# Pads in three pools, so that the activations' parts lie 64 bytes from the weights' parts modulo 256

## The chip, the cores and the metric

The kernel runs on one core of a Trainium2 chip. The metric is the device time of the whole program, in microseconds; before the change three runs gave 2711.12, 2712.39 and 2712.43 us. About 0.2% (5.4 us) is what a measurement of this kernel can tell from no change.

## The reference, cut to what matters

Three transformer-like blocks follow one another on a sequence of 256 tokens with 1024 features, all in float32. Nearly all the work is matrix products of the 256 tokens with weights that are read once from HBM:

```
def first_block(x, c, ...):
    mod = silu(c) @ w_ada + b_ada
    h = modulate(rms_norm(x, g), shift, scale)
    p = h @ w_in                        # Fourier mixing, convolution, gates
    ...
    x = x + gate * ((gate_a * y_a + gate_b * y_b) @ w_o)
    x = x + gate * expert_choice_moe(...)   # 16 experts, 32 tokens each

def second_block(x, p, ...):
    ...                                  # LRU branch, sparse attention, merge
    x = x + (gelu(conv(xn @ w_up[:, :3072])) * (xn @ w_up[:, 3072:])) @ w_down
    x = x + sigmoid(rms(x) @ w_ple_gate) * (p @ w_ple_proj)

def third_block(x, ...):                 # two layers
    x = x + 0.5 * swiglu(rmsnorm(x), w_gu, w_down)      # 1024 -> 2*2816 -> 1024
    x = x + mixer(rmsnorm(x))            # sparse, then sliding-window attention
    x = x + 0.5 * swiglu(rmsnorm(x), w_gu, w_down)
```

## The kernel before, in words

**Products.** Activations are kept with features on the 128 partitions: a tile `[128, 8, 256]` holds 1024 features of 256 tokens, 1024 bytes in each partition for each of the 8 feature blocks. To keep float32 accuracy with the faster float32r matmul, each operand is split into a high part and a low part (`wh`, `wl` of the weights, `xh`, `xl` of the activations; names such as `xgh`/`xgl`, `hh`/`hl` are such pairs), and three matmuls replace one. `lin_fm` (feature-major result, most of the kernel) issues for each block `k` and each half `f` of a 256-column unit of weights

```
self.mm(o, wh[:, k, c], xh[:, k, :], ...)   # weights are loaded, tokens move
self.mm(o, wh[:, k, c], xl[:, k, :], ...)
self.mm(o, wl[:, k, c], xh[:, k, :], ...)
```

All go through `mm` (L394). Each is a weight load of 128 columns (LDWEIGHTS, shown as PEld) and a matmul that streams 256 columns of the other operand; the load for the next matmul overlaps the stream of the current one. A unit of 1024 x 256 weights is 48 matmuls. `lin_tm` (token-major result) has the roles exchanged: it loads the activations' parts and streams the weights' parts.

**Weights.** `Stream` brings weights from HBM into slots of 16384 bytes per partition (`raw`), and `prep_one` and `settle` (L280 on ScalarE, L289 on VectorE) split each unit into `wh` and `wl`, which lie side by side in another slot (`w`). The slots are pools on the right side of SBUF, allocated downwards; six serve the dense parts, ten the experts.

**Activations.** Their tiles come from pools that are opened and closed as on a stack, left ones upwards and right ones downwards. What counts for the change is where a tile begins in its partition. In the program as the allocator lays it out before the change (addresses modulo 256):

| pool | side | holds | modulo 256 |
|---|---|---|---|
| slots | right | `raw`, `w` (`wh`, `wl`), tiles lent for attention (`lent`) | 224 |
| `act` (L2623), under the slots | right | `xgh`/`xgl`, `hh`/`hl` of the feed-forward parts, `yh`/`yl`, `QS` | 224 |
| `fixed` (`kn.fx`) | left | parameters, `xT`, sums, identity `identr` (192) | various |
| `big` (L381), after `fixed` | left | `z0`/`z1`, `xg0`/`xg1`, `mt0`/`mt1`, the experts' `ht`, `xe` | 0 |
| `act2`, `plein`, where `big` has closed | left | `hh`/`hl` of one group of a feed-forward part, `pT` | 0 |
| `mods` (L825), then `one` (L827), after `big` | left | `one`: `hh`/`hl`, `ybh`/`ybl`, `uf` (96); `yf` (0) | 96 |
| `three` in the last mixer | left | `KH`/`KL` | 160 |

Tiles of the matrix kind have rows of 1024 bytes, slots are 16384 bytes apart, and the halves `c` of a weight row lie 512 bytes apart, so the difference between any block of an activation tile and any block of a weight tile is the same modulo 256. One case matters below: `yf` lies in the same region of SBUF as the `act` tiles do later (from byte 109312 on), but at 0 modulo 256.

**Order.** The program is emitted in the order of the work, with queues written out by hand: `step` emits the matmuls of a unit and then older evictions; `Stream.pump` issues the DMAs on SyncE as slots come free. A feed-forward part (`ffn`) emits gate and up units by groups of 1024 hidden features, then the down products (`acc`) of the group before. Of each feed-forward part, of which there are five, the group `g == 1` has its `hh`/`hl` in `act2`, the others in `act`.

Of the kernel before, what the change touches and what calls it, by code (L numbers as in the profile page):

```python
# [8 lines left out]
F32 = mybir.dt.float32  # L9
# [6 lines left out]
P = 128  # L16
# [333 lines left out]
class Kern:  # L350
# [24 lines left out]
    def open_act2(self, ctx):  # L375
        p = ctx.enter_context(self.pool("act2"))
        self.act2 = lambda name, dt=F32R: p.tile([P, 8, S], dt, name=name, tag="act2", bufs=2)

    def open_big(self, ctx):
        self.bigctx = ctx.enter_context(ExitStack())  # L380
        p = self.bigctx.enter_context(self.pool("big"))  # L381
        self.big = lambda name, i, dt=F32R: p.tile([P, 8, S], dt, name=name, tag=f"big{i}", bufs=1)
# [362 lines left out]
def plan_one(kn):  # L745
    st, A = kn.st, kn.A
    ph = 1
    u = kn.u1 = {}
    Wa = A["w_ada"][0]

    def ada(q, c):

        u["ada", q, c] = st.raw(ph, 2, 2048, Wa[:, q * 2048:(q + 1) * 2048].rearrange("(p k) n -> p k n", k=8)[:, 2 * c:2 * c + 2], 2 if q == 0 else 1)

    Wi = A["w_in"][0]
    for a in ADA[:3]:
        ada(*a)
    u["u", 0] = st.linear(ph, Wi, 0, 8, 0)
    ada(*ADA[3])
    u["u", 1] = st.linear(ph, Wi, 0, 8, 256)  # L760
    rest = ADA[4:]
    n = 0

    def more():
        nonlocal n
        n += 1
        if n in ADA_AT:
            ada(*rest.pop(0))

    for j in range(4):  # L770
        for nm, c0 in (("v", 512), ("c", 2560), ("b", 1536)):
            u[nm, j] = st.linear(ph, Wi, 0, 8, c0 + j * 256)
            more()
    for j in range(8):
        u["g", j] = st.linear(ph, Wi, 0, 8, 3584 + j * 256)
        more()
    for j in range(4):
        u["wf", j] = st.linear(ph, A["w_fourier"][0], 0, 4, j * 256)
        more()
        u["wc", j] = st.linear(ph, A["w_conv_out"][0], 0, 8, j * 256)  # L780
        more()
    for j in range(4):
        u["wo", j] = st.linear(ph, A["w_o"][0], 0, 8, j * 256)


def plan_experts(kn):
    st, A = kn.st, kn.A
    kn.ue = {}
    for e in range(16):
        for nm in ("w_gate_e", "w_up_e"):  # L790
            W = A[nm][0, e].rearrange("(c p i) n -> c p (i n)", p=P, i=4)
            if e < 2:
                kn.ue[e, nm] = [st.rows(2, 2, 2048, W[c][:, h * 4096:(h + 1) * 4096], pair=False) for c in range(2) for h in range(2)]
            else:
                kn.ue[e, nm] = [st.rows(2, 4, 2048, W[c]) for c in range(2)]
        W = A["w_down_e"][0, e].rearrange("(c p i) n -> c p (i n)", p=P, i=8)
        halves = [W[c][:, h * 4096:(h + 1) * 4096] for c in range(2) for h in range(2)]
        kn.ue[e, "w_down_e"] = d = []
        if e < 2:
            d += [st.rows(2, 4, 1024, w, pair=(e, n) == (1, 3)) for n, w in enumerate(halves)]  # L800
        elif e < 15:
            d += [st.rows(2, 8, 1024, W[c]) for c in range(2)]
        else:
            d += [st.rows(2, 4, 1024, w, pair=False) for w in halves[:3]]
            if 2 in kn.stages:
                plan_two_first(kn, 0)
            d.append(st.rows(2, 4, 1024, halves[3], (2,), pair=False))
    if 2 in kn.stages:
        plan_two_first(kn, 1)
# [13 lines left out]
def block_one(kn, outer):  # L823
    nc, A, st, V, SC, G = kn.nc, kn.A, kn.st, kn.V, kn.SC, kn.G
    modp = outer.enter_context(kn.pool("mods"))  # L825
    with ExitStack() as ctx:
        pool = ctx.enter_context(kn.pool("one"))  # L827
        st.phase = 1
# [606 lines left out]
def plan_two(kn):  # L1435
    st, A = kn.st, kn.A
    ph = 3
    if "e" not in kn.stages:
        plan_two_first(kn, 0)
        plan_two_first(kn, 1)  # L1440
    u = kn.u2
    W = A["w_in_2"][0]
    o_q, o_k, o_v, o_qi, o_ga, o_gb = 2048, 3072, 3328, 3584, 4168, 5192
    col = dict(q=(W, o_q), lx=(W, 0), lg=(W, 1024), ga=(W, o_ga), gb=(W, o_gb), qi=(W, o_qi), k=(W, o_k), v=(W, o_v), lb=(A["w_lru_br_2"][0], 0))

    def add(key):
        w, c = col[key[0] if isinstance(key, tuple) else key]
        u[key] = st.linear(ph, w, 0, 8, c + 256 * (key[1] if isinstance(key, tuple) else 0))

    add("k")  # L1450
    u["rg"] = st.unit(ph, 8, 256, [((0, P), (0, P), A["lru_wa_2"][0].rearrange("n c d -> c n d")),
                                   ((0, P), (P, 256), A["lru_wx_2"][0].rearrange("n c d -> c n d"))])
    u["middle"] = [("lx", 1), ("q", 0), ("lx", 2), ("ga", 0), ("lx", 3), ("q", 1), ("ga", 1), "v", ("q", 2), ("ga", 2), ("q", 3), ("ga", 3)]
    for key in u["middle"]:
        add(key)
    for j in range(4):
        add(("lg", j))
    u["later"] = [("gb", 0), ("gb", 1), ("lb", 0), ("lb", 1), ("lb", 2), ("lb", 3), ("gb", 2), ("gb", 3)]
    for key in u["later"]:
        add(key)  # L1460
    for j in range(4):
        u["ab", j] = st.linear(ph, A["w_attn_br_2"][0], 0, 8, j * 256)
    for j in range(4):
        u["wo", j] = st.linear(ph, A["w_out_2"][0], 0, 8, j * 256)
    kn.ffn2 = plan_ffn(st, ph, A["w_up_2"][0], 3072, A["w_down_2"][0])
    for j in range(4):
        u["pg", j] = st.linear(ph, A["w_ple_gate_2"][0], 0, 8, j * 256)
    u["pp"] = st.linear(ph, A["w_ple_proj_2"][0], 0, 2, 0, D)
# [458 lines left out]
def ple_input(kn, pool):  # L1927

    nc, A = kn.nc, kn.A
    pin = pool.tile([P, 2, 256], F32, name="pin")  # L1930
    nc.gpsimd.dma_start(pin, A["p_2"][0, 0].rearrange("(t p) n -> p t n", p=P))
    kn.pT = [pool.tile([P, 2, S], F32R, name=f"pT{i}") for i in range(2)]

    def run():
        for _ in range(4):
            yield
        ps = kn.psB("pT")
        for f in range(2):
            for t in range(2):
                kn.T.transpose(ps[:, f * 256 + t * P:f * 256 + (t + 1) * P], pin[:, t, f * P:(f + 1) * P], kn.ident)  # L1940
        yield
        kn.split(*kn.pT, ps.rearrange("p (a b) -> p a b", a=2))
    kn.bgs.append(run())
# [629 lines left out]
def start_at(kn, gain):  # L2573

    kn.st.phase = 3
    kn.st.pump()
    with kn.pool("start") as pool:
        setup(kn, pool)
        params(kn, 0)
        load_rows(kn, pool, 1, len(kn.used), kn.nc.gpsimd)  # L2580
        params(kn, 1)
        kn.SC.activation(kn.identr, kn.ident, AF.Copy)
        turn_x(kn)
        for _ in prepare_two(kn, pool):
            pass
    nx = Next(kn, gain, at=kn.two_parts("xg"))
    for j in range(4):
        nx.pair(j)
    return nx
# [20 lines left out]
def build(tc, A, out, stages=(1, "e", 2, 3)):  # L2610
    with ExitStack() as ctx:
        kn = Kern(ctx, tc, A, out, stages)
        if 1 in stages:
            plan_one(kn)
        if "e" in stages:
            plan_experts(kn)
        if 2 in stages:
            plan_two(kn)
        if 3 in stages:
            plan_three(kn)  # L2620

        def open_act():
            actp = ctx.enter_context(kn.pool("act", "right"))  # L2623
            kn.act = lambda name, dt=F32R: actp.tile([P, 8, S], dt, name=name, tag="act", bufs=5)

        nx = None
        kn.open_big(ctx)
        if 1 in stages:
            with ExitStack() as outer:
                route = block_one(kn, outer)  # L2630
                if "e" in stages:
                    experts(kn, route, outer, 2 in stages)
                    nx = kn.follow
        open_act()
        kn.st.phase = 3
        kn.st.pump()
        if 2 in stages:
            if nx is None:
                nx = start_at(kn, lambda k: kn.col("mix_norm_2", k))
            nx = mixer_two(kn, nx)  # L2640
            kn.bigctx.close()
            with kn.pool("plein") as pool:
                ple_input(kn, pool)
                nx = ffn_two(kn, nx)
                nx = ple_two(kn, nx, lambda: Next(kn, lambda k: kn.col("ffn1_norm_3", k)))
        if 3 in stages:
            if 2 not in stages:
                nx = start_at(kn, lambda k: kn.col("ffn1_norm_3", k))
            return block_three(kn, nx)
        dump(kn)  # L2650
# [31 lines left out]
```

## Time and profile before

| | |
|---|---|
| median of three runs | 2712.39 us |
| profiled execution, its own time | 2713.4 us |
| its span, first to last instruction | 2711.6 us |
| PE (matmul) busy | 2318.2 us, 85% |
| VectorE busy | 1127.8 us, 42% |
| ScalarE busy | 908.9 us, 34% |
| GpSimd busy | 355.5 us, 13% |
| HBM read | 713.14 MB |

A matmul's duration in the profile includes its way through the array (283 ns for the usual one), and matmuls overlap; what counts for the time is the distance from one start to the next, which is read from the timeline, or from a stretch without gaps by dividing its length by the count of matmuls. A window counts every instruction that touches it, so that with durations of 283 ns and distances of 120 ns about two more are counted than start in it. Up to about 190 us the first block runs, to 1176 us the experts, to 1434 us the second block's mixer, to 1673 us its feed-forward part and what follows, then four feed-forward parts of the third block with a mixer after the first (1868 to 2045 us) and after the third (2412 to 2530 us).

### The profile page before, as it was taken

Reading aid. Unit: us, or ns where it says so; the run is one execution under the profiler, and the core shown is the slowest. Engines: PE = TensorE matmul, PEld = TensorE weight load, DVE = VectorE, ACT = ScalarE, POOL = GpSimd, SP = SyncE. Lnnn points to the kernel's source line nnn. Section 1 sums busy time; section 2 is a strip of 40 time slices with the busy share of each in tenths; the row PEclk is TensorE's granted clock in tenths of the full one; section 3 lists DMA queues with packets and bytes.
Section 4 is the critical chain, followed back from the end, with each engine's and each line's share of the span. In section 5 each row is a group of like instructions: output and inputs, shape, how many; then the busy total and the mean of one; then the engine's idle time right before and its main releaser. Section 6 shows DMA issues by size and latency. Waiting matters only on the chain. (4 is left out here: it accounts for less than half of the span.)

```text
span 2711.6 us, 39808 instructions
## 1 busy us (share of the span) xinstructions
PE 2318.2 (85%) x17635; PEld 1867.4 (69%) x17635; DVE 1127.8 (42%) x1324; ACT 908.9 (34%) x1223; POOL 355.5 (13%) x221
## 2 busy tenths in 40 slices
PE   7999756656666566699999999999999999998999
PEld 5988211111221111179899999999889999997998
DVE  5445000000000000059766666555785555558653
ACT  3343100000000000037845445434664344345533
POOL 0001000000000000002302112212222122130311
PEclk8999987787787777799999999999999999999999
DMA  9689999999999999984465555555345555552651
GB/s 326 233 284 373 390 432 430 431 432 430 430 431 430 431 432 428 431 275 133 133 207 180 180 184 173 177 172 182 88 125 182 179 184 184 177 159 84 197 180 70
DMA packets 262912, 717.15 MB, mean 264 GB/s; under 512 B 9827, under 2 KB 206676, under 8 KB 245460
## 3 DMA queue, kind: packets, MB, share of 16 engines
q1 hardware_dynamic: 258908, 709.62, 69.4%
q10 hardware_dynamic: 3000, 3.02, 0.5%
q8 instruction: 138, 2.26, 0.3%
q0 software_dynamic: 832, 1.97, 0.3%
q14 instruction: 34, 0.28, 0.0%
HBM read 713.14 MB, written 1.44 MB: 264 GB/s over the span
## 5 line engine op out<-in xcount | busy, mean ns | idle before, releaser
L289 DVE TENSOR_TENSOR w<-raw,w 128x2048 fp32r<-128x2048 f32 (+1 forms) x273 | 617.1, 2263 | 287.3 <-ACT w L280 287.2
L280 ACT ACTIVATE w<-raw 128x2048 fp32r<-128x2048 f32 (+1 forms) x273 | 509.6, 1869 | 587.2 <-DVE w L289 178.9
L394 PE MATMUL gu<-raw,xe 128*32 128x512 f32 x2048 | 349.4, 844 | 243.6 <-DMA raw<-in_w_up_e_dram 128.3
L394 PEld LDWEIGHTS gu<-raw,xe 128*32 128x32 f32 x2048 | 85.4, 146 | 506.4 <-issue 346.4
L394 PE MATMUL gate<-xgh,w 128*128 128x256 f32 x1792 | 332.5, 283 | 0.0
L394 PE MATMUL up<-xgh,w 128*128 128x256 f32 x1792 | 332.4, 283 | 0.0
L394 PE MATMUL acc<-hh,w 128*128 128x256 f32 x1792 | 322.1, 282 | 0.0
L394 PEld LDWEIGHTS up<-xgh,w 128*128 128x128 f32 x1792 | 283.5, 192 | 0.3
L394 PEld LDWEIGHTS gate<-xgh,w 128*128 128x128 f32 x1792 | 283.4, 192 | 0.0
L394 PEld LDWEIGHTS acc<-hh,w 128*128 128x128 f32 x1792 | 277.7, 190 | 0.0
L394 PE MATMUL gate<-xgl,w 128*128 128x256 f32 x896 | 254.5, 284 | 4.5 <-DVE xgl L412 4.5
L394 PE MATMUL up<-xgl,w 128*128 128x256 f32 x896 | 253.6, 283 | 0.0
L394 PE MATMUL acc<-hl,w 128*128 128x256 f32 x896 | 252.0, 281 | 0.0
L1275 DVE TENSOR_TENSOR sg<-sg,gu 128x512 f32<-128x512 f32 x16 | 11.0, 687 | 578.8 <-PE gu L394 578.8
L394 PE MATMUL py<-raw,hT 128*32 128x512 f32 x1024 | 150.5, 732 | 87.5 <-DMA raw<-in_w_down_e_dram 76.4
L2027 POOL TENSOR_TENSOR t<-t,tu 128x512 f32<-128x512 f32 x44 | 130.7, 2970 | 457.2 <-ACT t L2025 451.0
L394 PEld LDWEIGHTS gate<-xgl,w 128*128 128x128 f32 x896 | 171.9, 192 | 5.9 <-DVE xgl L412 5.9
L394 PEld LDWEIGHTS up<-xgl,w 128*128 128x128 f32 x896 | 172.0, 192 | 0.0
L394 PEld LDWEIGHTS acc<-hl,w 128*128 128x128 f32 x896 | 170.8, 191 | 0.0
L394 PEld LDWEIGHTS py<-raw,hT 128*32 128x32 f32 x1024 | 35.4, 130 | 190.3 <-DMA raw<-in_w_down_e_dram 92.5
L1283 ACT ACTIVATE hT<-ph 128x512 f32<-128x512 f32 x16 | 9.6, 597 | 356.5 <-PE ph L1281 356.5
L1246 POOL TENSOR_TENSOR ohs<-ohr,pr 128x128 f32<-128x128 f32 x32 | 12.1, 399 | 824.4 <-PE po L1248 818.8
(441 smaller groups left out, 3269.6 us busy)
## 6 DMA issues: line engine op xcount, KB each, us to landing
raw<-in_w_gate_e_dram SPq DMA_DIRECT2D x28, 4096.0 KB, 43.2
raw<-in_w_up_e_dram SPq DMA_DIRECT2D x28, 4096.0 KB, 43.5
raw<-in_w_down_e_dram SPq DMA_DIRECT2D x26, 4096.0 KB, 43.2
raw<-in_ffn_w_gu_dram SPq DMA_DIRECT2D x88, 1024.0 KB, 7.6
raw<-in_w_in_dram SPq DMA_DIRECT2D x36, 1024.0 KB, 8.8
raw<-in_w_up_dram SPq DMA_DIRECT2D x24, 1024.0 KB, 7.7
raw<-in_ffn_w_down_dram SPq DMA_DIRECT2D x12, 2048.0 KB, 7.9
raw<-in_w_down_e_dram SPq DMA_DIRECT2D x11, 2048.0 KB, 38.7
```

Source lines behind the costliest of these rows:

```text
L280: kn.nc.scalar.activation(wh, v, AF.Copy)
L289: self.kn.nc.vector.tensor_tensor(wl, v, wh, op=OP.subtract)
L394: self.nc.tensor.matmul(out, lhsT, rhs, start=start, stop=stop, skip_group_check=True)
L1246: G.tensor_tensor(src, ohr[:, t, None, e * 32:(e + 1) * 32].to_broadcast([P, 4, 32]), pr[:, t, e:e + 1, None].to_broadcast([P, 4, 32]), op ...
L1275: V.tensor_tensor(sg, sg, pu, op=OP.mult)
L1283: SC.activation(flat(hT), ph, AF.Copy)
L2027: G.tensor_tensor(t, t, tu, op=OP.mult)
```

## The change

A method `pad` allocates a tile of `n` bytes per partition in a pool and clears it on GpSimd (without a write the tile would not be there). It is called at three places: 160 bytes in `fixed` before `big` opens, 160 bytes at the start of `mods`, and 64 bytes in a pool of its own on the right just before `act` opens under the slots. So the tiles of `fixed` (of which the pad becomes the first), `big` and all that follows on the left move up by 160, `one` and the rest of block one by 320, and `act` moves down by 64: `act`, `big`, `act2`, `plein` and `one` all come to lie at 160 modulo 256, with the slots still at 224. No product, DMA or order of the work changes.

```diff
@@ -376,7 +376,12 @@
         p = ctx.enter_context(self.pool("act2"))
         self.act2 = lambda name, dt=F32R: p.tile([P, 8, S], dt, name=name, tag="act2", bufs=2)
 
+    def pad(self, pool, n):
+
+        self.G.memset(pool.tile([P, n // 4], F32, name="pad"), 0.0)
+
     def open_big(self, ctx):
+        self.pad(self.fx, 160)
         self.bigctx = ctx.enter_context(ExitStack())
         p = self.bigctx.enter_context(self.pool("big"))
         self.big = lambda name, i, dt=F32R: p.tile([P, 8, S], dt, name=name, tag=f"big{i}", bufs=1)
@@ -823,6 +828,7 @@
 def block_one(kn, outer):
     nc, A, st, V, SC, G = kn.nc, kn.A, kn.st, kn.V, kn.SC, kn.G
     modp = outer.enter_context(kn.pool("mods"))
+    kn.pad(modp, 160)
     with ExitStack() as ctx:
         pool = ctx.enter_context(kn.pool("one"))
         st.phase = 1
@@ -2620,6 +2626,7 @@
             plan_three(kn)
 
         def open_act():
+            kn.pad(ctx.enter_context(kn.pool("pad", "right")), 64)
             actp = ctx.enter_context(kn.pool("act", "right"))
             kn.act = lambda name, dt=F32R: actp.tile([P, 8, S], dt, name=name, tag="act", bufs=5)
```

## Rows read from the trace of the kernel before

**Rows 1.** The page: span, and TensorE's granted clock in 40 slices.

```profile
span 2711.6 us, 39808 instructions
...
PEclk8999987787787777799999999999999999999999
```

**Rows 2.** Windows: length, busy (count) of PE, PEld, DVE, ACT, POOL; clock, DMA share, GB/s.

```profile
0.00:180.00 180.00, 161.06 (x1254) 140.04 (x1255) 87.00 (x121) 71.12 (x83) 1.01 (x6) 0.95 0.78 270
...
250.00:1176.00 926.00, 591.44 (x3535) 198.95 (x3534) 43.91 (x89) 43.33 (x72) 15.38 (x35) 0.80 1.00 426
...
1690.10:1828.30 138.20, 138.20 (x1154) 138.20 (x1153) 73.66 (x55) 58.92 (x47) 29.74 (x10) 1.00 0.54 179
...
1868.30:2045.00 176.70, 167.34 (x1322) 151.53 (x1322) 129.62 (x187) 100.79 (x240) 51.53 (x38) 0.98 0.44 126
...
2412.50:2530.00 117.50, 106.91 (x844) 99.28 (x843) 92.53 (x147) 65.11 (x143) 28.19 (x19) 0.97 0.45 124
```

**Rows 3.** Timeline of PE, an up unit from `act`: start, length, matmul, count.

```profile
1500.10 0.28 PE L394 MATMUL up<-xgl,w 128*128 128x256 f32 x1
...
1501.18 0.28 PE L394 MATMUL up<-xgl,w 128*128 128x256 f32 x1
```

**Rows 4.** Windows: down products whose activations lie in `act2`.

```profile
1597.19:1619.80 22.61, 22.61 (x194) 22.61 (x193) 13.48 (x14) 10.52 (x10) 3.97 (x2) 1.00 0.57 186
```

**Rows 5.** Timeline of PE: `one` at 96, `yf` at 0, and weights streamed past `big`.

```profile
102.34 0.28 PE L394 MATMUL psA<-hl,w 128*128 128x256 f32 x1
...
104.12 0.28 PE L394 MATMUL psA<-hl,w 128*128 128x256 f32 x1
...
185.28 2.87 PE L394 MATMUL psA<-yf,w 128*128 128x256 f32 x23
...
1207.74 3.00 PE L394 MATMUL psA<-w,xg 128*128 128x256 f32 x24
```

**Rows 6.** Timeline of PE, scores of the last mixer: first and last of 12.

```profile
2446.64 0.29 PE L394 MATMUL S<-KH,QS 128*128 128x256 f32 x1
...
2447.94 0.29 PE L394 MATMUL S<-mask,identr 128*128 128x256 f32 x1
```

**Rows 7.** Weight loads by line, 1500 to 1590 and 1597.5 to 1619.5 us: mean ns second.

```profile
L394 PEld LDWEIGHTS up<-xgh,w 128*128 128x128 f32 x188 | 29.8, 192 | 0.0
...
L394 PEld LDWEIGHTS acc<-hh,w 128*128 128x128 f32 x125 | 19.0, 188 | 0.0
```

**Rows 8.** Timeline of PEld: loads whose matmuls stream two columns only.

```profile
1177.58 0.97 PEld L394 LDWEIGHTS nps<-sums,nacc 128*128 128x128 f32 x8
```

**Rows 9.** Matmuls by line: count, busy us, mean ns, idle us before.

```profile
L394 PE MATMUL gate<-xgh,w 128*128 128x256 f32 x1792 | 332.5, 283 | 0.0
...
L394 PE MATMUL acc<-hh,w 128*128 128x256 f32 x1792 | 322.1, 282 | 0.0
L394 PE MATMUL gate<-xgl,w 128*128 128x256 f32 x896 | 254.5, 284 | 4.5 <-DVE xgl L412 4.5
...
L394 PE MATMUL acc<-hl,w 128*128 128x256 f32 x896 | 252.0, 281 | 0.0
...
L394 PE MATMUL psA<-hh,w 128*128 128x256 f32 x640 | 117.0, 283 | 0.0
...
L394 PE MATMUL un<-w,xgh 128*128 128x256 f32 x480 | 91.5, 291 | 7.4 <-DVE w L289 7.4
...
L394 PE MATMUL psA<-yh,w 128*128 128x256 f32 x128 | 24.7, 290 | 0.0
...
L394 PE MATMUL psA<-xgh,w 128*128 128x256 f32 x128 | 23.7, 284 | 0.0
```

**Rows 10.** Timeline of POOL: a small memset, and the stretch in which `act` opens.

```profile
0.74 0.10 POOL L714 MEMSET nhalf<- 128x8 f32 x1 [0.29 <-POOLq L2669]
...
1099.91 0.76 POOL L1246 TENSOR_TENSOR ohs<-ohr,pr 128x128 f32<-128x128 f32 x2 [57.58 <-PE po L1248]
1181.16 0.53 POOL L1543 MEMSET KI<- 128x512 f32 x1 [80.49 <-issue]
```

## The prediction, made before the changed kernel was run

> **What bounds the kernel now.** I read the page first, for the granted clock: full over the second half of the span, lower only among the experts [rows 1]. Then the windows, stage by stage, for the engine that never rests. In the experts (250 to 1176 us) that is the DMA: share 1.00 at 426 GB/s, with PE busy 591 of 926 us. In the first block the DMA share is 0.78 and PE is busy 161 of 180 us, so neither rules alone. In a feed-forward stretch such as 1690 to 1828 us PE is busy for the whole 138.20 us while VectorE has 73.66 and the DMA share is 0.54: only PE counts there. In the two attention mixers of the third block PE is busy 167 of 177 and 107 of 118 us, with gaps that belong to others [rows 2].
>
> So the question is how fast PE turns over matmuls. The starts say it: in an up unit the xl product of one block begins at 1500.10 and that of three blocks on at 1501.18 us, 1.08 us for nine matmuls, 120 ns each [rows 3]. The window of 138.20 us gives the same (1154 counted, some two of them begun before: 138.20/1152 = 120.0 ns) [rows 2]. All have activations and weights at the same place modulo 256, distance 0.
>
> The same instructions go faster elsewhere, at the same full clock. Distance below is the streamed operand's place less that of the operand loaded meanwhile, modulo 256.
>
> - +32: the down products from act2, 192 matmuls in 22.61 us: 117.8 ns [rows 4]. There are five such stretches.
> - +32 again, but in the part of SBUF where act lies later: yf, 23 matmuls in 2.87 us, less 0.28 for the last one's length, over 22: 117.7 ns [rows 5].
> - 128: block one, 15 matmuls between 102.34 and 104.12 us: 118.7 ns [rows 5].
> - -32: weights streamed past big, (3.00 - 0.28)/23 = 118.3 ns [rows 5].
> - -64, -32 and +32 in turn: the last mixer's scores, where KH at 160 streams while QS at 224 is loaded, 1.30 us over 11 distances: 118.2 ns [rows 6].
>
> The yf row tells that it is the place modulo 256 and not the region. The -32 row tells that it is the difference and not the streamed operand's own place, for there the streamed weights lie at 224 as in the slow case. The weight loads say the same from their side: 192 ns at distance 0, 188 at +32 [rows 7]. So two reads that go on together cost something, a little more at distance 0 than at any other distance seen.
>
> **The change part by part.** After it, lin_fm streams from 160 and loads from 224, distance -64; lin_tm has +64. No stretch of the trace runs steadily at either, so its matmul distance is bounded. From below by 111 ns: eight 128-column loads take 0.97 us where only two columns are streamed, (0.97 - 0.19)/7 with a load's own 0.19 us, so the load alone does not let it fall further [rows 8]. From above by 122 ns: 120.0 is the worst steady row, and the unevenness of the starts in block one (102.34 to 104.12 us, steps of 0.35 to 0.36 us per three) leaves room for some 2 ns more. I take 118.2: the scores, the one row with -64 in it, give that, and it lies between the +32 rows and the 128 row, its neighbours on either side.
>
> *Distance 0 becomes 64.* Gate has 1792 + 896 matmuls, up by the code as many, acc as many [rows 9]; of acc, five stretches of 192 are at +32 already: 3 x 2688 - 960 = 7104. The ple gate (xgh 128, and half as many xgl) and the LRU branch (yh 128, with yl) add 2 x 192 [rows 9]: 7488. They run where PE has no gaps, so each 1.8 ns is on the path: -13.5 us. What could be late next there is VectorE, busy 53% of the stretch, and the DMA at 54% [rows 2]; neither comes near with PE 1.5% faster. The mixers' un products (480 and half as many low ones, 720) gain the same per matmul, but gaps follow in which the gain can vanish [rows 2, 9]; I take half: -0.6 us.
>
> *Distance 32 becomes 64.* act2's 960, and 240 of mt and pT by the code: +0.4 ns each, +0.5 us. The second block's xg products stand between 117.8 and 118.3 now [rows 4, 5] and come to 118.2: nothing, bounds from the same 111 and 122.
>
> *Distance 128 becomes 64.* Block one has 640 + 320 such (hh, hl) [rows 9] and some 300 more by the code, -0.4 ns each; half of it passes the DMA: -0.3 us. The experts' matmuls read big at a new place too, but the DMA's 1.00 covers them with 335 us of idle PE [rows 2]. Products with both operands in slots (wo and those with lent tiles) stay at 0.
>
> *Added: three memsets on GpSimd.* A small one takes 0.10 us [rows 10]. Two are issued at the start, where POOL is idle. The third must wait until the slot that lay there has been read for the last time; behind it on POOL stands KI's memset at 1181.16 us, after 80 us of rest [rows 10]. KI's region was read by its former owners until just before, so the pad's wait, over when the last expert's weights are used, ends earlier. Nothing; with that cover gone 0.1 us. VectorE, ScalarE and the DMAs meet the moved tiles at other places; for a slower or faster pass I see no row, the slots that carry most bytes stay, and their slack in the PE stretches covers some per cent: 0.
>
> Sum: -13.5 - 0.6 + 0.5 - 0.3 = -13.9 us. From the profiled execution's 2713.4 us that is 2699.5; the median of the runs lies 1.0 below that execution, so 2698.5, said as 2698.
>
> By the Trainium skill's page "TensorE: Matmul & The Clock Gate", section Part 2 (back-to-back issue gap), a matmul of 256 columns at full clock needs 256/2.4 + 2.5 = 109 ns; an estimate from it: if distance 64 freed the stream wholly, 7488 x 10.9 ns = 81 us would go. No row here reaches that.
>
> **The rivals.**
>
> *A, 64 is clear of the clash.* If the cost of two reads together has a hole at a quarter of 256, matmuls come down to the middle of 111 and 118, 114.5 ns. Then 7488 x 5.5 = 41, un 2, act2, mt and pT 1200 x 3.3 = 4, xg half of 1176 x 3.6 = 2, block one half of 1260 x 4.1 = 3: 52 us less, 2660. For it: 111 against 117.7 shows that some 7 ns of cost are left at +32. Against: 32, 128 and -32 differ by 1 ns among themselves, no sign of a hole, and the scores with -64 among them show none either. 13%.
>
> *B, nothing that can be measured.* Distance 64 has a steady pace of 119.2 to 120.5, or what goes faster is not the distance. Then 2711. For it: distance 0 and 128 differ by just 1.3 ns. Against: five stretches at 117.8 in between stretches at 120.0. The skill's page "SBUF — State Buffer", section "Who interferes with whom", gives TensorE two independent read ports, for the moving operand and for the weights, and says that TensorE never waits for anyone: by that rule this change moves nothing. The trace disagrees, 120.0 against 117.8 ns at one clock. That the pads do not do what they say (a pool that lands elsewhere) would fall under B too. 18%.
>
> *C, slower.* At 64 each load meets the stream as at 0, and later lines of it again, and the pace locks above: 122 ns. Then 7488 x 2.0 = 15, un 1, act2, mt and pT 1200 x 4.2 = 5, xg 2, block one 2: 25 us more, 2737. It decides from some 120.8 ns on. For it: distance 0 shows that a pace can lock at its worst (every step 0.12 us [rows 3]). Against: all other rows lie below 0. 7%.
>
> **How the numbers follow.** The forecast has 62%; its own range is 117.4 to 119.0 ns: 7488 x 2.6 with the rest in proportion gives 2691, 7488 x 1.0 less what act2 gives back 2706. The range takes in B and A down to 115 ns, and leaves out the lower half of A and C: 2664 to 2713. Faster than before by over 0.2% (5.4 us, about what a measurement of this kernel can tell) is the forecast and A, 75%; within it B, 18%; slower C, 7%.
>
> **What would show it.** In the profile after: the feed-forward windows with more matmuls per microsecond, 118 ns from start to start; the length of the weight loads there 188 and not 192 ns; act2's stretches at the same pace as their neighbours, no longer faster; the experts' stretch unchanged, and POOL's third memset in its long rest before KI. The prediction is wrong if gate and up units run at 120 or below 117 ns, or if new gaps open in front of PE and swallow what it gained.

## The result, and the profile after

The changed kernel took 2674.47 us (median of 4 runs, 2671.46 to 2680.8) against 2711.76 for the kernel before on the same chip: ratio 0.9866, 95% interval 0.9846 to 0.9885. 37 us went, where 14 were forecast; the time lies inside the range and far from the point. The profiled execution was the longest of the four, 2680.8 us, so the traces below account for 32.6 us of span.

The page, against [rows 1]:

```profile
span 2679.0 us, 39811 instructions
...
PE 2279.6 (85%) x17635; PEld 1828.3 (68%) x17635; DVE 1128.2 (42%) x1324; ACT 909.7 (34%) x1223; POOL 354.6 (13%) x224
...
PEclk8999987777887777789999999999999999999999
```

Both spans were then cut at the same matmuls of the program, so that each window holds the same work. First windows of the kernel before (length, busy and count of PE, PEld, DVE, ACT, POOL; granted clock, DMA share, GB/s): block one, the experts, then the five feed-forward streams (a stream is the long run of matmuls of one feed-forward part; the third and fourth are in one window) and the two mixers of the third block between them.

```profile
0.00:272.90 272.90, 249.65 (x1965) 221.55 (x1965) 134.28 (x204) 105.04 (x122) 11.47 (x16) 0.95 0.83 302
272.90:1172.90 900.00, 569.28 (x3422) 180.99 (x3424) 31.26 (x55) 32.27 (x53) 11.34 (x30) 0.80 1.00 427
...
1434.20:1642.80 208.60, 208.60 (x1746) 208.60 (x1745) 130.34 (x145) 104.07 (x111) 38.98 (x18) 1.00 0.56 183
...
1673.00:1868.10 195.10, 191.64 (x1597) 191.03 (x1596) 106.07 (x90) 85.63 (x76) 42.01 (x17) 1.00 0.52 172
1868.10:2029.30 161.20, 152.21 (x1201) 136.94 (x1200) 116.07 (x176) 91.12 (x231) 47.21 (x35) 0.98 0.41 117
2029.30:2412.40 383.10, 382.73 (x3194) 382.12 (x3193) 208.01 (x163) 166.97 (x143) 83.41 (x31) 1.00 0.56 181
2412.40:2508.30 95.90, 85.97 (x675) 78.89 (x674) 76.42 (x135) 51.20 (x130) 19.93 (x15) 0.96 0.39 102
2508.30:2711.60 203.30, 196.69 (x1630) 195.18 (x1628) 101.94 (x80) 86.29 (x79) 42.69 (x18) 0.99 0.45 149
```

The same windows of the kernel after:

```profile
0.00:267.80 267.80, 244.01 (x1969) 214.76 (x1970) 134.47 (x204) 105.16 (x122) 11.60 (x18) 0.96 0.85 308
267.80:1167.30 899.50, 566.89 (x3422) 180.01 (x3424) 31.23 (x54) 32.17 (x53) 11.45 (x31) 0.80 1.00 427
...
1427.30:1625.10 197.80, 197.80 (x1746) 197.80 (x1745) 130.49 (x146) 104.27 (x111) 39.39 (x18) 1.00 0.59 193
...
1654.70:1840.20 185.50, 182.03 (x1597) 181.42 (x1596) 106.23 (x90) 85.84 (x76) 41.38 (x17) 1.00 0.54 181
1840.20:2003.90 163.70, 153.26 (x1202) 137.82 (x1201) 116.22 (x176) 91.26 (x231) 47.42 (x35) 0.97 0.42 116
2003.90:2381.10 377.20, 376.53 (x3192) 375.77 (x3192) 207.79 (x162) 166.73 (x141) 83.17 (x31) 1.00 0.57 184
2381.10:2478.50 97.40, 87.18 (x675) 79.98 (x674) 76.68 (x135) 51.47 (x131) 18.96 (x15) 0.95 0.39 100
2478.50:2679.00 200.50, 193.69 (x1630) 192.18 (x1628) 101.96 (x80) 86.44 (x79) 42.85 (x18) 0.99 0.45 151
```

The feed-forward stages give 10.8 + 9.6 + 5.9 + 2.8 = 29.1 us, block one 5.1, the experts 0.5, what lies between 1.9; the two mixers give back 2.5 and 1.5. VectorE, ScalarE and GpSimd are as busy as before. The unevenness is the finding: 1746 matmuls of the first stream gained 10.8 us, while the third and fourth together, nearly twice as many, gained 5.9, at the same distance and the same clock.

A window of 100 us inside each of the five streams shows why. The count in the second column gives the pace: two or three of the counted matmuls began outside, so 884 or 885 is 113.3 ns from start to start, 851 or 852 is 117.8, and 836 is the 120.0 of before.

```profile
1475.00:1575.00 100.00, 100.00 (x885) 100.00 (x884) 68.55 (x75) 51.47 (x55) 18.59 (x7) 1.00 0.59 191
1700.00:1800.00 100.00, 100.00 (x884) 100.00 (x884) 54.96 (x40) 44.09 (x34) 21.95 (x8) 1.00 0.56 188
2050.00:2150.00 100.00, 100.00 (x852) 100.00 (x851) 53.05 (x39) 41.59 (x32) 21.71 (x7) 1.00 0.56 180
2235.00:2335.00 100.00, 100.00 (x852) 100.00 (x851) 52.17 (x40) 42.44 (x32) 20.09 (x7) 1.00 0.58 187
2515.00:2615.00 100.00, 100.00 (x851) 100.00 (x851) 52.99 (x39) 41.55 (x32) 21.81 (x7) 1.00 0.57 190
```

So distance 64 has two steady paces, called low (113.3) and high (117.8) below. (Streamed less loaded, the distance is -64, which is 192 modulo 256; for the changed kernel the text goes on saying 64, and the table by distance lists it as 192.) A stream takes one near its start and keeps it: streams one and two are low, three to five high, with one value over some 1500 matmuls each. The nine-matmul step of [rows 3] is now 1500.13 to 1501.15 us, 113.3 ns each:

```profile
1500.13 0.28 PE L399 MATMUL up<-xgl,w 128*128 128x256 f32 x1
...
1501.15 0.28 PE L399 MATMUL up<-xgl,w 128*128 128x256 f32 x1
```

The down products from `act2` [rows 4] go at their neighbours' pace: in the first stream 180 matmuls in 20.40 us (113.3), in the third 120 in 14.13 us (117.8):

```profile
1590.23:1610.63 20.40, 20.40 (x182) 20.40 (x181) 11.55 (x9) 10.06 (x10) 2.67 (x1) 1.00 0.55 184
2160.10:2174.23 14.13, 14.13 (x122) 14.13 (x121) 6.46 (x5) 5.41 (x4) 1.19 (x1) 1.00 0.56 187
```

The weight loads [rows 7] tell the two paces apart. Before, at distance 0, every load took 192 ns, those for the `xgl` products too (first line below). Now every load takes 188 ns in the low streams (second line, 1500 to 1590 us), while in the high ones (third and fourth line, 2060 to 2150 us) one load of every three still takes 192 ns, here that of the `xgl` products:

```profile
L394 PEld LDWEIGHTS gate<-xgl,w 128*128 128x128 f32 x93 | 17.9, 192 | 0.0
...
L399 PEld LDWEIGHTS gate<-xgl,w 128*128 128x128 f32 x80 | 15.0, 188 | 0.0
...
L399 PEld LDWEIGHTS gate<-xgh,w 128*128 128x128 f32 x192 | 29.7, 188 | 0.0
...
L399 PEld LDWEIGHTS gate<-xgl,w 128*128 128x128 f32 x96 | 18.4, 192 | 0.0
```

The third memset sits where it was expected, between the last expert and KI's memset [rows 10]:

```profile
1162.02 0.11 POOL L381 MEMSET pad<- 128x16 f32 x1 [66.78 <-PE py L399]
1175.61 0.52 POOL L1549 MEMSET KI<- 128x512 f32 x1 [13.47 <-DVE xT L1319]
```

### The profile page after: what moved, and what is told of

Its sections match the earlier page's. It is cut to its first block, busy times and chain, and to the rows that moved or that the text cites. A ratio compares the mean times of both kernels' runs of the same rounds, so it can differ in the third digit from the quotient of the medians.

```text
span 2679.0 us, 39811 instructions
## 1 busy us (share of the span) xinstructions
PE 2279.6 (85%) x17635; PEld 1828.3 (68%) x17635; DVE 1128.2 (42%) x1324; ACT 909.7 (34%) x1223; POOL 354.6 (13%) x224
## 5 line engine op out<-in xcount | busy, mean ns | idle before, releaser
L399 PE MATMUL up<-xgh,w 128*128 128x256 f32 x1792 | 322.1, 280 | 0.0
L399 PE MATMUL gate<-xgh,w 128*128 128x256 f32 x1792 | 321.6, 279 | 0.0
L399 PE MATMUL acc<-hh,w 128*128 128x256 f32 x1792 | 313.3, 279 | 0.0
L399 PEld LDWEIGHTS up<-xgh,w 128*128 128x128 f32 x1792 | 276.4, 188 | 0.3 <-DVE w L289 0.3
L399 PEld LDWEIGHTS gate<-xgh,w 128*128 128x128 f32 x1792 | 276.2, 188 | 0.0
```

The lines of the kernel that those rows point to most:

```text
L399: self.nc.tensor.matmul(out, lhsT, rhs, start=start, stop=stop, skip_group_check=True)
```

## The experiments

Two questions: is it the distance modulo 256 and nothing else about the new places, and what picks low or high? Paces below are worked out from the starts of the matmuls in each trace, sorted by the distance that the program's addresses give.

**The changed kernel again.** No edit; it ran in four more sets, beside other kernels.

> The changed kernel as it is, once more. In its profile every long stream of matmuls at distance 64 ran at one of two steady paces, 113.3 or 117.8 ns from start to start: the five feed-forward parts at 113, 113, 118, 118, 118. Theory 1: which of the two is drawn when a stream starts anew and then kept, so another execution has another row of fast and slow parts, and a time some 6.4 us (1440 matmuls x 4.4 ns) per part away from the first's: anything from 2661 to 2694 us. Theory 2: the pace is settled by where the tiles of a part lie, and then the row is 113, 113, 118, 118, 118 again and the time 2680.

> The changed kernel once more, on the chip of the two kernels with added matmuls. Theory 1 (the start of a stream draws its pace): the median lies between 2662 (all five feed-forward streams at 113.3 ns) and 2700 us (all at 117.8), and with the pattern of both looks so far, two at 113.3 and three at 117.8, at 2675 +- 5. Theory 2 (the place in the program fixes the pace): the profile shows the same pattern again, 113.3, 113.3, 117.8, 117.8, 117.8, and 2671 to 2681 us.

> The changed kernel beside it, for the comparison on one chip: 2671 to 2688 us, each feed-forward stream at 113.3 or 117.8 ns, the first at 113.3 and the last three mostly at 117.8 if the three looks so far are typical.

> The changed kernel beside them, for the comparison on one chip: 2664 to 2688 us, streams one and two at 113.3 ns and three to five at 117.8, or one of them changed.

Measured: 2676.64 (one run); 2678.81 (2678.41 to 2688.13); 2678.55 (2664.16 to 2684.12); 2679.06 us (2676.4 to 2681.92). In five profiles the streams were low, low, high, high, high four times. In the second of these sets stream two was high as well, its stage 192.0 us in place of 185.5 and the execution 2688.13 us long:

```profile
1700.00:1800.00 100.00, 100.00 (x852) 100.00 (x851) 52.09 (x40) 42.41 (x32) 20.15 (x7) 1.00 0.55 182
```

So the pace is neither fixed by the place in the program nor evenly random: mostly the same, sometimes not, 6.5 us for one stream, and neither of the pure theories holds. For the execution of 2688.13 us that is most of what it lies above its set's median; that the spread of the runs without a profile (2664.16 to 2684.12 in the third set) has the same cause is likely, not shown.

The two mixers of the third block, which gave back 4.0 us in the first profile, took 160.8 and 95.6 us in the first set's profile, 163.6 and 97.5 in the second's, 161.0 and 97.1 in the third's and 162.0 and 95.6 in the fourth's, against 161.2 and 95.9 in the one profile before: from a gain of 0.7 to a loss of 4 us, varying from one execution to the next.

**One side of the pads alone.** The right pad only (distance 64 for the streams, 32 for `act2`), and the left pads only (the streams keep 0, `act2` gets 64):

```
e2_act:  open_act():  + kn.pad(ctx.enter_context(kn.pool("pad", "right")), 64)
e3_left: open_big():  + self.pad(self.fx, 160)
         block_one(): + kn.pad(modp, 160)
```

> Only the 64 bytes under the slots; no pads on the left, so act lies at distance 64, act2 and big at 32, block one at 128 as before. If the gain is act's matmuls (7488 from 120.0 to a mean of 116): 30 us less than before, 2682, give or take 7 by the draw of the two paces. If the left pads carry as much as the right one: 2694 or more.

> Only the two pads on the left; act stays at distance 0, act2, big and block one come to 64. By the distances: block one's 1140 matmuls from 118.8 to 115 with half behind the DMA, act2, mt and pT's 1200 from 117.8 to 116, the xg products from 118 to 116.5: some 2 + 2 + 1 = 5 us less than before, 2707, and the act parts at 120.0 ns. If the left pads are half of the gain: 2693.

Measured: right pad 2687.63 us (ratio 0.9908, 0.9894 to 0.9923), left pads 2704.64 (0.9971, 0.9960 to 0.9981). With the left pads a stream stays at 120.0 and its `act2` stretch goes low, in all five streams (here 189 matmuls in 21.42 us):

```profile
2050.04:2150.84 100.80, 100.80 (x843) 100.80 (x841) 54.63 (x41) 41.11 (x32) 22.18 (x7) 1.00 0.56 185
2173.52:2194.94 21.42, 21.42 (x192) 21.42 (x190) 10.50 (x8) 8.33 (x7) 3.15 (x1) 1.00 0.47 152
```

With the right pad stream three is high (840 in 98.94 us), passes `act2` at distance 32 (189 in 22.05 us, 116.7, not the 117.8 of [rows 4]) and comes out low (180 in 20.40 us):

```profile
2050.03:2148.97 98.94, 98.94 (x843) 98.94 (x842) 53.95 (x39) 41.68 (x32) 21.83 (x7) 1.00 0.55 182
2162.28:2184.33 22.05, 22.05 (x192) 22.05 (x190) 10.50 (x8) 8.48 (x7) 3.16 (x1) 1.00 0.46 150
2184.91:2205.31 20.40, 20.40 (x182) 20.40 (x181) 13.33 (x16) 13.74 (x17) 6.07 (x3) 1.00 0.73 235
```

All five streams came out of distance 32 low, four of them having gone in high. So the gain follows the distance of the operands concerned, and a spell at another distance can change a stream's pace. The two gains, 24.7 and 7.7 us, sum to 32.4; the full change gave 33 to 37.

**A different distance for each weight slot.** The weights in the six slots lie at 192, 160, 128, 96, 64 and 32 modulo 256, `act` at 32, `big` at 0; then all slots' contents 16 bytes further.

```
 slot():  tile([P, n + 8 * (1 + self.paired)], ...)[:, OFF:OFF + n]     (8 elements are 32 bytes)
e4_steps:   OFF = 0        (the kernel before, without pads)
e5_steps16: OFF = 4
```

> The kernel before without pads, but with 32 bytes more in each slot, so that the weights of slots 0 to 5 lie at 192, 160, 128, 96, 64 and 32 modulo 256 and act at 32: one program with distances 96, 128, 160, 192, 224 and 0, changing from unit to unit as the slots take turns. Theory 1 (distance modulo 256, with two paces at some distances): within one stream the pace steps with the slot: 120.0 at 0; 113.3 or 117.8 at 192; 118.5 or 120 at 128; 118 at 224; 119 to 120 at 96; 160 unknown, 113 to 120. Theory 2 (place in SBUF, not distance): one pace through all units of a part. Total by theory 1 about 2703, 2690 to 2712.

> The slots of the stepped kernel moved on by 16 bytes: act at 32, big at 0, the six weight slots at 208, 176, 144, 112, 80 and 48 modulo 256, so that every distance between stream and load is an odd multiple of 16. Theory 1 (the distance modulo 256 fixes the paces that a stream can hold, in steps of 32 bytes or finer): each odd multiple of 16 holds one or two paces of its own between 113 and 120 ns, and a unit with distance 48 or 80 shows whether 113.3 ns goes on beside 64; if the grain is 32 bytes, 80 behaves as 64 or 96 does (113.3 and 117.8, or 120.0), and 208 as 192 or 224. Theory 2 (only multiples of 64 or whole 32-byte lines matter): 16 bytes more make every row of odd multiples the mean of its neighbours. Time by theory 1: 2690 to 2706 us, near the 2701 of the kernel without the 16 bytes.

Measured: 2701.27 and 2705.71 us, one run each. Pace by distance (units of some 40 to 192 matmuls at one distance, rounded to thirds of a ns):

```
  0   120.0 (33 units)           16   120.0 (2 of 3)
 32   116.7 (2), 117.7 (2)       48   116.7 (16 of 17)
 64   113.3 (5), 117.7 (14)      80   118.0 to 118.3 (31 of 33)
 96   120.0 (32)                112   120.0 (19), 118.3 (6), 116.7 (4)
128   118.7 (31)                144   120.0 (34 of 43)
160   117.3 (18), 118.7 (20), 120.0 (3)    176   118.7 (39 of 44)
192   113.3 (23), 117.7 (21)    208   117.7 (27 of 38), 123.3 (4)
224   118.3 (37 of 40)          240   118.3 (31 of 33)
```

Three windows of 42 matmuls each in the first of the two kernels, one unit each, show distance 96, 192 at the high pace, and 64 at the low; a window of 47 matmuls in the second shows distance 208 at 123.3:

```profile
1479.16:1484.20 5.04, 5.04 (x44) 5.04 (x43) 3.67 (x5) 3.40 (x4) 1.33 (x1) 1.00 0.41 134
1484.92:1489.86 4.94, 4.94 (x44) 4.94 (x43) 3.80 (x6) 2.06 (x4) 0.66 (x1) 1.00 0.76 248
1598.56:1603.32 4.76, 4.76 (x45) 4.76 (x43) 3.29 (x6) 2.39 (x4) 0.15 (x1) 1.00 0.72 244
...
2617.95:2623.74 5.79, 5.79 (x49) 5.79 (x48) 2.29 (x1) 0.84 (x1) 0.00 (x0) 1.00 0.77 254
```

The pace changes unit by unit with the slot, inside one unbroken stream, so the distance decides which paces a stream can hold. It is the difference and not the place of either operand: 0 gives 120.0 with both at 224 before and with both at 32 here, and 192 gives the same two paces with 160 against 224 in the changed kernel and with 32 against 96 here. The grain is finer than 32 bytes: 80 is neither 64 nor 96, 48 has one pace of its own. No distance of the sixteen goes below 113.3, and only 64 and 192 reach it. Nor is distance 0 the slowest: four units at 208 took 123.3. A unit at distance 64 that came straight from 192 kept the pace it had: 3 of 3 low from low, 3 of 3 high from high. So a state is carried from matmul to matmul.

**Eight matmuls more near the start of a stream.** If a state is carried, a few matmuls at another distance should move it. At 16 places, ahead of the second unit after each interruption, eight 256-column matmuls were added whose sum the unit overwrites. They stream the identity at distance 32, the identity at 128, or the unit's own first operand at 192:

```
 lin_fm():
+  if self.fresh == 1 and start and cut is None and nk == 8 and not self.fine:
+      for _ in range(8):
+          self.mm(ps[:, 0:256], wh[:, 0, 0:P], X, True, False)
e6_prod32, e7_prod128:  X = self.identr[:, None, :].to_broadcast([P, 2, P])
   (e6_prod32 also moves identr by 96 bytes)
e9_prod192:             X = xh[:, 0, :]
```

> The changed kernel with eight more 256-column matmuls, which stream the identity at distance 32 from the loads, ahead of the second gate or up unit after each interruption of the stream; their sums are overwritten by the unit that follows. Theory 1 (at distance 64 a stream keeps either 113.3 or 117.8 ns, whichever it falls into at its start, and a spell at distance 32 drops it into the lower, as after act2 in the kernel with the right pad alone): all five feed-forward streams run at 113.3 ns; three of five that were at 117.8 gain 1530 x 4.4 ns = 6.8 us each, 20 us, less 16 x 8 x 0.115 = 15 us of added matmuls, some of them beside other waits: 2668 to 2674 us. Theory 2 (the pace belongs to the place in the program, as both looks at the changed kernel gave the same streams the same pace): streams one and two at 113.3, three to five at 117.8 as before, and the time is 2676 + 15 = 2691 us.

> The same added matmuls in the same places, but with the identity 96 bytes further, at distance 128 from the loads. Theory 1 (the spell at distance 32 sets the pace): at 128 the added matmuls set it otherwise or not at all, so the streams behind them stay a mix of 113.3 and 117.8 ns: 2680 to 2695 us. Theory 2 (any insertion shifts the start and draws anew): the mix is the same as in the kernel with the identity at 32, whatever that one shows.

> The same eight added matmuls in the same 16 places, but each is the unit's own first product once more, so the distance is 192 in them as in the stream. Theory 1 (a stream that has held another distance without a break enters 64 or 192 at 113.3 ns; a stream that starts at it after a gap takes either pace): the added matmuls already hold whatever the start drew, so the five feed-forward streams are a mix again, one to three at 113.3 ns, and the time is 2680 to 2695 us. Theory 2 (any eight matmuls more at the start do it): four or five at 113.3 ns, 14 or 15 of the 16 places, 2670 to 2676 us as with the identity at 32 or at 128.

Measured: 2670.84 (0.9849, 0.9834 to 0.9864), 2673.44 (one run) and 2688.59 us (one run). With the identity at 32 or at 128 the stream was low behind 14 of the 15 places where a pace could be read, in either kernel (of the five streams in four and in five); with the own operand the pattern was low, low, high, high, high as without. The third stream with the identity at 128, and with the own operand:

```profile
2050.00:2150.00 100.00, 100.00 (x884) 100.00 (x884) 53.99 (x40) 44.51 (x34) 21.80 (x7) 1.00 0.59 193
```

```profile
2050.00:2150.00 100.00, 100.00 (x851) 100.00 (x851) 53.93 (x39) 41.30 (x32) 21.80 (x7) 1.00 0.56 184
```

So an insertion by itself does nothing; it must stand at another distance. That distance 32 was needed was wrong: 128 does it too.

**Four, and where.** Eight at 16 places cost 128 matmuls. First four, at distance 128, ahead of each stream's first up unit; then four, and eight, behind the last interruption, the fp32 matmuls of `rps` (and the transposes of `pT` in the first stream); then four in streams three to five alone.

```
+    def prime(self, w, ps, n): ...      (n matmuls as above, distance 128)
e10_prime4:  lambda: (kn.prime(w, ps, 4) if p == 0 else None, kn.lin_fm(w, nx.x, ps))
e12_prime_late, e13_prime8 (in lin_fm, for gate and up of the feed-forward only):
+  if prime and self.fresh == 1:
+      for _ in range(4):                (8 in e13_prime8)
e14_prime4_last3:
+      for _ in range(4 if self.primed > 3 else 0):
```

> Four added matmuls in place of eight, at distance 128, ahead of the first up unit of the five feed-forward streams only. Theory 1 (a short spell at another distance sets the pace): all five streams at 113.3 ns; against the kernel with 16 x 8 added matmuls some 108 fewer, 12 us, less where a wait hid them: 2658 to 2668 us, under the changed kernel's 2675 to 2679. Theory 2 (the spell must be long enough for the streams to settle, and four matmuls are too few): the mix of the changed kernel, 2674 to 2682 us.

> The four added matmuls at distance 128 once more, now behind the last interruption of each feed-forward stream (behind the matmuls of rps, and in the first stream behind those of pT as well): 6 places, 24 matmuls, 2.8 us. Theory 1 (four matmuls at another distance set the pace to 113.3 ns, and a later interruption by fp32 matmuls lets it be drawn anew, which is why four ahead of rps did not help): all five feed-forward streams at 113.3 ns, 2678.5 - 3 x 6.8 + 3 = 2661 us, range 2655 to 2667. Theory 2 (four are too few, or the streams' place in the program decides): the mix of the changed kernel, 2674 to 2698 us.

> Eight added matmuls in place of four at the same 6 places. Theory 1 (the phase that loads and stream have at the entry decides, and eight at distance 128 lead to 113.3 ns from either pace, four turn one pace into the other): all five feed-forward streams at 113.3 ns; 2675.9 - 2 x 6.8 + 24 x 0.118 = 2665 us, range 2660 to 2669. Theory 2 (chance): a mix, each stream at 113.3 or 117.8 ns, 2670 to 2690 us.

> The four added matmuls ahead of streams three, four and five only. Theory 1 (four turn one pace into the other, and the start draws 113.3 for streams one and two and 117.8 for the others, as in four of five looks at that pattern): all five at 113.3 ns; 2675.9 - 2 x 6.8 - 12 x 0.118 = 2661 us, range 2655 to 2668. Theory 2 (chance): a mix, 2668 to 2690 us.

*Four ahead of the first up unit*: 2695.63 us (0.9937, 0.9924 to 0.9949), a miss for both theories; all five streams were high. The trace shows that the four did work, and that the gain was lost again. In the fifth stream the unit behind them goes low (45 matmuls in 5.12 us, the first ones slower), then `rps` comes (two fp32 matmuls that spread the norm's factors over the partitions), and the stream behind it is high (450 in 53.08 us):

```profile
2500.44 0.72 PE L399 MATMUL up<-identr,w 128*128 128x256 f32 x4
...
2500.99:2506.11 5.12, 5.12 (x48) 5.12 (x46) 4.30 (x3) 1.78 (x1) 2.69 (x1) 1.00 1.04 330
2506.81:2559.89 53.08, 53.08 (x453) 53.08 (x452) 29.10 (x23) 25.95 (x21) 14.16 (x5) 1.00 0.62 202
```

In nine traces (the five of the changed kernel and those with added matmuls at 192, four early, four late, and four in the last three) this crossing of `rps` can be read 45 times. A stream that was low before it was high behind it in 18 of 18. From high it went low 15 times and stayed high 12: low in streams one and two, high in three to five. So nothing was drawn behind `rps`: streams one and two changed over (15 times from high, 3 from low), and three to five came out high 27 times of 27, from either pace. What differs from one execution to the next is the pace ahead of it.

*Four behind the last interruption*: 2675.92 us (0.9866, 0.9850 to 0.9883), where 2661 was forecast. The time lies in the second theory's range, but neither theory has the pattern. Streams three to five went from high to low, and streams one and two from low to high. Stream two: 36 matmuls in 4.08 us ahead of the four (113.3), 450 in 53.00 us behind them (117.8). Stream three: 117.9 ahead, 450 in 51.00 us behind (113.3).

```profile
1682.51:1686.59 4.08, 4.08 (x38) 4.08 (x37) 3.05 (x3) 3.17 (x3) 0.81 (x1) 1.00 1.02 341
1688.00:1741.00 53.00, 53.00 (x452) 53.00 (x451) 29.35 (x24) 23.52 (x20) 12.69 (x4) 1.00 0.53 169
2035.10:2039.35 4.25, 4.25 (x39) 4.25 (x38) 2.55 (x2) 3.81 (x4) 1.45 (x1) 1.00 0.02 4
2041.08:2092.08 51.00, 51.00 (x452) 51.00 (x451) 27.73 (x23) 22.42 (x18) 12.71 (x4) 1.00 0.62 205
```

Four matmuls at distance 128 thus turn one pace into the other, both ways, 6 of 6. Chance would not do that, and the next two runs were forecast from it.

*Eight there*: 2665.02 us (2662.78 to 2667.06; 0.982, 0.9806 to 0.9833), forecast 2665; all five streams low, behind two places where the stream came low and four where it came high. *Four in the last three only*: 2663.13 us (2656.69 to 2666.12; 0.9811, 0.9798 to 0.9825), forecast 2661; all five low. Its third and fifth streams:

```profile
2050.00:2150.00 100.00, 100.00 (x885) 100.00 (x884) 56.02 (x41) 43.09 (x33) 23.11 (x8) 1.00 0.55 182
...
2515.00:2615.00 100.00, 100.00 (x885) 100.00 (x884) 55.93 (x40) 42.59 (x33) 21.72 (x7) 1.00 0.53 180
```

Both are faster than the changed kernel on the same chip (2676.4 to 2681.92): no run of theirs overlaps with it (on another chip one run of the changed kernel took 2664.16), and 2663.13/2679.06 is 0.994. Twelve matmuls that compute nothing save 16 us. This version beats both kernels; that it does so in every run rests on the start drawing low in streams one and two, which it did in four of five profiles of the changed kernel. The one with eight does not need that.

## Why the prediction was wrong

The bound was right: the feed-forward streams wait for PE alone, and what PE gained there came out of the time whole, 29.1 us. The failed step is the pace at the new distance, as the prediction put it: "I take 118.2: the scores, the one row with -64 in it, give that". Distance 64 does not have one pace but two, and 118.2 is neither. Over the profile's 7540 matmuls from `act` the mean was 116.0 ns: 7488 x 4.0 = 30 us for the term put at 13.5. The step failed in two ways.

- It read one number from twelve matmuls at mixed distances [rows 6], and interpolated between neighbours at 117.7 to 118.7 [rows 4, 5]. The pace is no smooth function of the distance: 120.0 at 96, 113.3 at 64, 116.7 at 48.
- It took a row's pace as the distance's own. The traces show that a pace belongs to a distance and a carried state together. The +32 rows, 117.8 five times over, were such a case: with the right pad alone the same stretches held 116.7. Steadiness over 192 matmuls looked like certainty and was one of two states.

Against the profiled execution (2699.5 forecast, 2680.8 measured) the 18.7 us missed are: 16.7 in the feed-forward stages (12.4 forecast with `act2`, 29.1 measured), 4.8 in block one, less 2.8 in the rest, where the mixers gave back 4.0.

- *Block one*: "half of it passes the DMA", 0.3 us. Measured 5.1: its 1139 matmuls at distance 64 have a mean of 114.9 ns (gaps left out), 118.8 before, so 1260 x 3.9 = 4.9 us would go if nothing hid any of it. The half was wrong too.
- *act2*: +0.4 ns each was forecast; the stretches took their stream's pace, 116.0 in the mean, 1.8 less. That they would go at their neighbours' pace was right.
- *The un products and gaps behind*: the mixers of the third block together vary by 4.7 us from profile to profile, more than this term; open.
- *Weight loads*: 188 and not 192 ns was the sign given. It came true in the low streams alone; in the high ones a third of the loads kept 192.
- *Experts, memsets*: 900.0 to 899.5 us, and POOL's rest, as forecast.

Of the rivals, A had the right kind of cause at the wrong weight: "64 is clear of the clash", 114.5 ns and 2660 us. The low pace is 113.3, and with all five streams low the measured time is 2663. It got 13% because the rows showed "no sign of a hole". The low bound of 111 had left room for it, and the range reached to 2664, which is why it held the time. B falls: kernels that differ only in places in SBUF run the same matmuls at 120.0, 117.8 and 113.3 ns at full granted clock. By the Trainium skill's page "SBUF — State Buffer", section "Who interferes with whom", TensorE's two read ports are independent and it never waits for anyone, so the pads would move nothing. The runs disagree: the pace went from 120.0 to 113.3 ns with nothing but places changed. C falls: nothing at 64 was above 118, though 123.3 at 208 shows that a distance can be slower than 0. By the Trainium skill's page "TensorE: Matmul & The Clock Gate", section Part 2 (back-to-back issue gap), the gap of an isolated matmul of 256 columns at full clock is 109 ns; no run's steady pace reached that, the lowest is 113.3.

What stays open: what the carried state is, and why it comes in two values at 64. The runs show that it is kept, turned and lost in a repeatable way, and that the high pace goes with one long load in three; no view shows the reads themselves. Nor is it shown why `rps` leaves a high stream low in streams one and two and high in the others.

## What to carry to other kernels

When PE is the bound and each matmul loads new weights, the place of the streamed operand relative to the next weights modulo 256 bytes can be worth a few per cent of the pace; here 64 or 192 was best, and 0, 96 and at times 208 worst, for 64 or 160 bytes of pad. Read the pace stream by stream, not as a mean: two streams of equal work at one clock with different counts per 100 us were here the sign of a state to win, and the length of the loads, sorted by product, was another. And where an untried setting lies between rows that were measured, its bounds belong in the forecast with more weight than the interpolation.

## What the runs showed of the hardware that was not expected

- Start-to-start pace of 128x128 by 256-column fp32r matmuls at full granted clock, by distance modulo 256: 120.0 ns at 0 and 96; 118.7 at 128; 118.3 at 224; 117.3, 118.7 or (3 units of 41) 120.0 at 160; 117.7 or (4 units of 38) 123.3 at 208; 116.7 or 117.7 at 32; 113.3 or 117.8 at 64 and 192.
- In the changed kernel (192 in the table) the pace is kept over some 1500 matmuls, and survives the step from one weight slot to the next.
- Weight loads there take 188 ns at the low pace; at the high one, one of every three takes 192; at distance 0 all do.
- Four matmuls at distance 128 turn it (9 of 9: 6 from high to low, 3 from low to high); eight lead to the low one (28 of 30 places with eight at 32 or 128, then 6 of 6); eight at the stream's own distance leave the pattern as it was.
- A crossing of two fp32 matmuls (`rps`) turned the low pace into the high one in 18 of 18; 15 of these lie in streams three to five, which came out high from the high pace as well (12 of 12).
